# Feature blocks of the latents in another order, and queries and keys stored in DRAM by row tile

## The chip, the core and the metric

The kernel runs on one core of one Trainium2 chip. The metric is device time in microseconds (us); the figure for the kernel before is the median of three runs. Engines are named as in the profile: PE is TensorE's matmuls and PEld its weight loads, DVE is VectorE, ACT is ScalarE, POOL is GpSimd, SP is SyncE, which here only issues DMAs. PSUM banks hold 512 float32 columns on 128 partitions.

## The reference, cut to what matters

The model has two layers over 256 context tokens and 2048 latent tokens of width 1024, all in float32. The change touches the first (even) layer, up to its softmax attention:

```python
h  = rms_norm(x, norm_g[i]) * (1 + scale) + shift       # scale, shift from silu(c) @ ada_w + ada_b
hc = rms_norm(cx, norm_g[i]) * (1 + c_scale) + c_shift  # the context's own
lat = split_cols(jnp.dot(h, w_in), EVEN_SPLITS)         # 768 query latents, 256 key/value latents, 32 rotary key, ...
q = jnp.dot(rms_norm(q_lat, q_norm), w_uq)              # 8 heads of 64 plain and 32 rotary features
kv = jnp.dot(rms_norm(kv_lat, kv_norm), w_ukv)          # 8 heads of 64 key and 64 value features
k = concat(kv[..., :64], k_rope)                        # one rotary key for all heads
q, k = rms_norm(q, q_gain), rms_norm(k, k_gain)         # then axial rotation of the last 32
p = softmax(q @ k.T * scale)                            # 2048 queries on 2304 keys, 256 context queries on 256
```

Beside it the layer has a gated linear attention (GLA) on other columns of `w_in`, and a second (odd) layer with neighbourhood attention follows. The modulation of the second layer uses the same conditioning, so its rows (`ada_w[1]`) can be computed at any time.

## The kernel before, in words

Matmul operands are float32 values split into a high and a low part, and a full product is three matmuls: high by high, high by low, low by high. The 2304 tokens are 18 row tiles of 128 (`NT`; the first two are context). A list scheduler puts each engine's instructions in order from the order in which the program issues them, from dependences and from its own estimate of times; `issue_after` pins an instruction behind another one. Tiles come from pools by tag with a number of buffers (`bufs`), and a new tile waits until the old one with the same buffer is free. The profiled execution goes through these stages:

**Start** (0 to 37 us). The first modulation rows (`ada_first`), the first weights.

**The latents** (`even_latent`, lines 405 to 597; 37 to 347 us). The transposed input is worked in six feature blocks of tokens (`BLOCKS0`, line 403), 256, 256, 512, 512, 512 and 256 wide. For a block, `load` brings x; `stats` squares it on ACT (L108 is the helper of every ACT operation), POOL adds the squares, DVE adds the last one with the epsilon (line 435, tile acc), and one matmul with a matrix of ones (line 438, tile st) sums over partitions; ACT takes logarithm and exponential, DVE corrects the root (to line 446, tile R). `modulate` multiplies by R (line 458), applies scale and shift on ACT, splits into hhi and hlo (line 461). `block` multiplies two of the eight 128-column weights at a time (48 matmuls, line 487, tile gm, four banks). `evict` takes a result out: ACT copies the high part and squares, DVE forms the low part (line 502, tile lev, four buffers), and two DMAs write both to the DRAM array LT, the high part on ACT's queue and the low part on SP's. `rope_keys` makes the rotary key: eight products of 32 output columns (line 516, tile rp), which accumulate in pairs into four column groups of TensorE, over x, k and the weight Tr. `rows` turns the sums of squares and the rotary key into token rows (tile tp) with some DVE work. Block 0 goes one weight at a time. In the loop over blocks, `load(b + 2)`, `stats(b + 1)`, `modulate(b + 1)` and `rope_keys(b + 1)` are issued together after the first pair of weights of block b, and `rows(b)` at its end; the scheduler moves them from there.

In the same stage eight remaining modulation rows are made (`ada_steps`, line 276; eight jobs). A job streams 2 MB of `ada_w` through DVE in eight steps of two instructions (lines 286 and 288, tiles adac), then has two matmuls with a pick matrix (line 293, tile tp), and `ada_row` adds the bias row (tile adab) and turns or writes the result. From block 1 on, half a job is issued after each pair of weights, all behind the last load of x.

**The up-projection** (`even_up`, lines 599 to 736; 359 to 654 us). ACT and DVE first split the weights w_uq and w_ukv. Then for each row tile, `up(t)` multiplies the latents, read back from LT, normalises and rotates (tiles qn and kn), `fetch(t + 2)` loads ahead, and `fin(t - 2)` transposes queries and keys (line 701, four transposes per half tile of four heads), scales and splits them into the staging tile qkhl (ACT the high part through L108, DVE the low part, line 705), which has two buffers, and writes the halves to DRAM with three DMAs on SP's queue: high and low plain features (line 709) and both rotary parts. There are four half tiles per row tile (queries, keys; heads 0 to 3, 4 to 7). The arrays are QA and KA, (part, head, feature, token), and QC and KC, (head, part, feature, token), so a row of one feature is contiguous over tokens. At the end of the stage `fin` of the last two tiles runs beside products of the next stage (`first`).

**Maxima and the rest of w_in** (`even_rest` with `maxes`, lines 746 to 811; 654 to 1176 us). For each head, `mk` holds the high keys of all tokens and `mq` the queries of six tiles, each loaded by two DMAs; products (line 799, tile mx) and DVE maxima (line 800) run woven into big matmuls.

**Attention woven with GLA** (`even_attention`, lines 1108 to 1295; 1176 to 2000 us). SP loads keys (akh), low keys (akl), values and, per query block, queries (aq) through a helper `dma` (line 1120): five DMAs for a piece of keys, three for low keys, seven for a query block. GLA's loads (gu, line 889) stand in the same queue; POOL works on gu at line 851 and TensorE at 859.

**The odd layer** (2000 to 3663 us), which the change leaves alone.

These few lines carry the order and the writes (lines 583 to 592 and 707 to 711):

```python
                for n, ms in enumerate(groups):
                    block(b, sp, ms)
                    if b and n == 0:
...
                            r = stats(b + 1, sp)
                            modulate(b + 1, r)
                            rope_keys(b + 1, sp)
                    if b:
                        with self.tc.issue_after(self.xload.ins):
                            next(ada, None)
```

## Time and profile before

| | |
|---|---|
| median of 3 runs | 3670.68 us (3665.3 to 3672.92) |
| the profiled execution's own time | 3664.74 us |
| its span in the trace | 3662.9 us |
| mean granted clock of TensorE | 0.979 of full speed |
| DMA packets, bytes | 438411, 555.85 MB, mean 152 GB/s |
| HBM read, written | 354.09 MB, 198.17 MB |

The page first gives the busy time of each engine, then the span in 40 slices (here 91.6 us each), where a digit is the busy share in tenths; PEclk is the clock that the throttle granted to TensorE, also in tenths. A view by windows gives the busy time and the number of instructions of each engine in a stretch, then mean clock, DMA share and GB/s; it can be asked for one tile or line alone. In the view of waits a row "PE st L438 <- DVE acc L435: 8.1, 2, 4.9" reads: TensorE's instructions of line 438 stood 8.1 us in all for VectorE's line 435, two times, the longest 4.9 us. In a list of instructions the columns are start, duration, engine, line, operation, tiles and shapes, and with "x2" how many records there are in one row. An issue row of SPq gives how many DMAs, their time in the queue's engine (lowest, median and highest in ns), from when to when. A queue's row has packets, MB and the share of time of 16 DMA engines.

### The profile page before, as it was taken

What the parts mean: (1) busy time and instruction counts of PE and PEld (TensorE: products, weight loads), DVE (VectorE), ACT (ScalarE), POOL (GpSimd) and SP (SyncE); (2) the same over time, 40 slices, a digit from 0 to 9 for tenths busy, and PEclk for the clock granted to TensorE, in tenths of its full rate; (3) what the DMA queues carried; (4) which work ended last, traced back from release to release, by engine and by line L of the source; (5) the groups of instructions that cost most, each with busy time, mean ns of one, the idle gap of its engine ahead of it and who ended that gap; (6) DMA issues with size and microseconds to landing.
All of it is one profiled execution on the core that took longest, in us unless ns stands there. A gap on an engine that the chain in (4) does not pass through costs nothing. (4 is left out here: it accounts for less than half of the span.)

```text
span 3662.9 us, 53768 instructions
## 1 busy us (share of the span) xinstructions
PE 3514.9 (96%) x19388; PEld 2654.4 (72%) x19388; DVE 2374.6 (65%) x4649; ACT 1387.6 (38%) x2371; POOL 1305.7 (36%) x1382
## 2 busy tenths in 40 slices
PE   8898897999999999999999999999899999999899
PEld 5566776888888566666555887888788887655577
DVE  5774665688887577777885435444577784666732
ACT  5433444111111454455664214444432222555510
POOL 3223352010101133322220224333344442888863
PEclk9898998999999999999999999999999999999999
DMA  8565777322222434243533645455744446888672
GB/s 288 160 189 159 237 216 199 105 89 74 83 70 78 115 93 124 67 132 106 181 119 99 201 141 156 141 156 158 224 149 133 142 126 174 219 221 218 197 236 96
DMA packets 438411, 555.85 MB, mean 152 GB/s; under 512 B 36009, under 2 KB 313081, under 8 KB 431986
## 3 DMA queue, kind: packets, MB, share of 16 engines
q1 hardware_dynamic: 358130, 451.98, 42.1%
q0 software_dynamic: 22032, 63.00, 5.6%
q10 hardware_dynamic: 57984, 37.43, 3.3%
q8 instruction: 154, 2.52, 0.3%
q14 instruction: 111, 0.91, 0.1%
HBM read 354.09 MB, written 198.17 MB: 151 GB/s over the span
## 5 line engine op out<-in xcount | busy, mean ns | idle before, releaser
L800 DVE TENSOR_REDUCE mm<-mx 128x1 f32<-128x512 f32 (+1 forms) x656 | 389.5, 629 | 84.6 <-PE mx L799 76.7
L108 ACT ACTIVATE apt<-st 128x1024 f32<-128x1024 f32 (+1 forms) x296 | 300.0, 1014 | 315.1 <-PE st L1269 300.3
L1276 DVE TENSOR_TENSOR acc<-acc,apt 128x1024 f32<-128x1024 f32 x256 | 340.6, 1331 | 80.0 <-ACT apt L108 60.7
L1269 PE MATMUL st<-aq,akh 64*128 64x512 f32 x1728 | 313.6, 410 | 1.1 <-ACT apt L108 0.7
L1179 PE MATMUL av<-apt,av 128*64 128x512 f32 x1152 | 265.8, 598 | 0.0
L799 PE MATMUL mx<-mk,mq 96*128 96x512 f32 (+1 forms) x656 | 236.6, 374 | 3.2 <-DMA mq<-QC 3.2
L1766 POOL TENSOR_TENSOR oacc<-oacc,opt 128x576 f32<-128x576 f32 (+5 forms) x192 | 222.8, 1183 | 36.8 <-ACT rl L108 16.6
L1885 DVE TENSOR_TENSOR opt<-st,tab 128x64 f32<-128x64 f32 (+10 forms) x576 | 144.5, 317 | 140.1 <-PE st L1727 63.7
L1269 PE MATMUL st<-aq,akl 64*128 64x512 f32 (+1 forms) x1152 | 231.5, 392 | 0.0
L1269 PEld LDWEIGHTS st<-aq,akh 64*128 64x128 f32 x1728 | 153.7, 186 | 82.7 <-ACT apt L108 29.3
L1643 DVE CUSTOM_DVE_ANT_1 mx<-mx,mtab 128x217 f32<-128x217 f32 (+12 forms) x576 | 184.0, 338 | 39.7 <-PE mx L1637 30.5
L1179 PEld LDWEIGHTS av<-apt,av 128*64 128x64 f32 x1152 | 76.3, 136 | 135.3 <-issue 134.3
L108 ACT ACTIVATE u<-gm 128x352 f32<-128x352 f32 (+1 forms) x86 | 44.4, 517 | 334.2 <-PE gm L133 216.4
L108 ACT ACTIVATE opt<-opt 128x930 f32<-128x930 f32 (+8 forms) x130 | 104.3, 805 | 107.5 <-DVE opt L1885 102.8
L799 PEld LDWEIGHTS mx<-mk,mq 96*128 96x128 f32 x656 | 121.4, 188 | 15.0 <-issue 3.6
L1269 PEld LDWEIGHTS st<-aq,akl 64*128 64x128 f32 (+1 forms) x1152 | 112.8, 185 | 23.1
L131 PE MATMUL gm<-w1h,hhi 128*128 128x512 f32 x288 | 116.7, 405 | 7.4 <-ACT onat L108 7.4
L131 PE MATMUL gm<-w0h,hhi 128*128 128x512 f32 x288 | 116.2, 403 | 1.9 <-DVE hhi L353 1.9
L132 PE MATMUL gm<-w1l,hhi 128*128 128x512 f32 x288 | 115.3, 400 | 0.0
L133 PE MATMUL gm<-w1h,hlo 128*128 128x512 f32 x288 | 114.5, 398 | 0.0
L212 POOL TENSOR_TENSOR oss<-oss,mhalf 128x8 f32<-128x8 f32 x68 | 112.4, 1654 | 5.1
L133 PE MATMUL gm<-w0h,hlo 128*128 128x512 f32 x288 | 114.0, 396 | 0.0
(592 smaller groups left out, 9757.9 us busy)
## 6 DMA issues: line engine op xcount, KB each, us to landing
q<-Q SPq DMA_DIRECT2D x48, 512.0 KB
H<-x ACTq DMA_DIRECT2D x36, 512.0 KB
x<-H SPq DMA_DIRECT2D x34, 512.0 KB
wraw<-ada_w SPq DMA_DIRECT2D x64, 256.0 KB
wraw<-w_od SPq DMA_DIRECT2D x64, 256.0 KB
K1t<-okt POOLq DMA_DIRECT2D x32, 512.0 KB, 7.5
kt<-K1t SPq DMA_DIRECT2D x32, 512.0 KB
mtab<-rpb_q SPq DMA_DIRECT2D x16, 899.0 KB
```

The costliest lines, as they stand in the source:

```text
L108: return self.nc.scalar.activation(out, in_, func, **kw)
L131: self.nc.tensor.matmul(out, lh(k), rh(k), start=start and j == 0, stop=False)
L132: self.nc.tensor.matmul(out, lh(k), rl(k), start=False, stop=False)
L133: yield self.nc.tensor.matmul(out, ll(k), rh(k), start=False, stop=stop and j == n - 1)
L799: mm = nc.tensor.matmul(ps[:, :w], q[:A_QK, (t % 6) * P : (t % 6) * P + P], k[:A_QK, k0 : k0 + w], start=True, stop=True)
L800: nc.vector.tensor_reduce(out=m[:, t, n : n + 1], in_=ps[:, :w], axis=AX.X, op=ALU.max)
L1179: mm = nc.tensor.matmul(O[j, nb][i * 64 : i * 64 + 64, :w], V[j, kt // TT][:, kt % TT, i * 64 : i * 64 + 64], pts[:, i, :w], start=n == 0, ...
L1269: mm = nc.tensor.matmul(ps[:, o // 64, :w], k[o : o + r, kb, kq], Q[o : o + r, qb, :w], start=m == 0, stop=m == 4)
L1276: added = nc.vector.tensor_tensor(out=acc[:, :, :w], in0=a[:, :, :w], in1=pts[:, :, :w], op=ALU.add)
L1643: nc.vector.tensor_tensor_reduce(out=s, in0=s, in1=tb[:, ri : ri + rn, ci : ci + cn], scale=1.0, scalar=-3e38, op0=ALU.add, op1=ALU.max, a ...
L1766: self.psum = nc.gpsimd.tensor_tensor(out=a, in0=a, in1=pts[:, :, a0 - r0 : a1 - r0, :], op=ALU.add)
L1885: bias = nc.vector.tensor_tensor(out=pt[:, d[0], d[1]], in0=ps[:, d[0], d[1]], in1=tabs[j][i][:, ri : ri + rn, ci : ci + cn], op=ALU.add)
```

## The change

It has two parts.

**The latents.** The blocks are 256, 256, 256, 512, 512, 512 wide. `stats` becomes a generator with two stops: the squares and their sum for block b + 2 are issued after the second pair of weights of block b, and product, logarithm and correction after the third pair; R gets two buffers. `rows(b - 1)` and `modulate(b + 1)` are issued after the first pair, `rope_keys(b + 1)` after the third, `load(b + 2)` at the block's start; all of these are pinned behind the last matmul of the pair. The eight products of `rope_keys` are chained by `issue_after` in the order second half first, groups 3, 0, 1, 2. The modulation jobs are separate generators, and a list `turn` says after which pair of which block each starts (and the one before it ends); from block 0 to block 5 there are nine such places. The bias row of `ada_row` takes its tile from tag lev, which has four buffers, where it had its own.

**Queries and keys in DRAM.** QA, KA, QC and KC become one array QK with axes (queries or keys, row tile, half of the heads, feature, head, part, token in tile). A half tile's staging tile, 96 features by 4 KB, is written by one DMA. All reads go through a new helper `heads`, whose pieces are the 128 tokens of one tile, 512 bytes. `mk` and `mq` take one DMA where they took two, a piece of keys six where it took five, low keys four for three, a query block twelve for seven.

The diff, cut to its core:

```diff
-        br = self.tl(sp, [2, 512], "adab", bufs=1)
+        br = self.tl(sp, [2, 512], "lev", bufs=4)
...
-    BLOCKS0 = [(0, CTX), (CTX, 256), (512, 512), (1024, 512), (1536, 512), (2048, 256)]
+    BLOCKS0 = [(0, CTX), (CTX, 256), (512, 256), (768, 512), (1280, 512), (1792, 512)]
...
+                yield
...
-                r = self.tl(sp, [P, w], "R", bufs=1)
+                r = R[b] = self.tl(sp, [P, w], "R")
...
-                return r
+                yield
...
-            def modulate(b, r):
-                q0, w = self.BLOCKS0[b]
+            def modulate(b):
+                (q0, w), r = self.BLOCKS0[b], R.pop(b)
...
-                for h in range(2):
-                    for n in range(4):
-                        nc.tensor.matmul(ps[n * 32 : n * 32 + 32, :w], wr[:, h * 4 + n, :], xb[:, h * 4 + n, :w], start=h == 0, stop=h == 1)
+                mm = None
+                for h in (1, 0):
+                    for n in (3, 0, 1, 2):
+                        with self.tc.issue_after(mm.ins) if mm else ExitStack():
+                            mm = nc.tensor.matmul(ps[n * 32 : n * 32 + 32, :w], wr[:, h * 4 + n, :], xb[:, h * 4 + n, :w], start=h == 1, stop=h == 0)
...
-            ada = self.ada_steps([(0, 4), (0, 5)] + [(1, b) for b in range(6)], sp, pp, "tp")
+            jobs = [self.ada_steps([j], sp, pp, "tp") for j in [(0, 4), (0, 5)] + [(1, b) for b in range(6)]]
+            turn = [(0, 3), (1, 1), (2, 1), (3, 0), (3, 2), (4, 0), (4, 2), (5, 0), (5, 2)]
...
-            r = stats(1, sp)
-            modulate(1, r)
-            rope_keys(1, sp)
-            load(2)
+            for _ in stats(1, sp):
+                pass
+            modulate(1)
...
-                if b == 0:
-                    groups = [(m,) for m in range(M)]
-                else:
-                    groups = [(m, m + 1) for m in range(0, M, 2)]
+                groups = [(m, m + 1) for m in range(0, M, 2)]
+                if b + 2 < nb:
+                    load(b + 2)
...
-                    block(b, sp, ms)
-                    if b and n == 0:
-                        if b + 2 < nb:
-                            load(b + 2)
-                        if b + 1 < nb:
-                            r = stats(b + 1, sp)
-                            modulate(b + 1, r)
-                            rope_keys(b + 1, sp)
-                    if b:
-                        with self.tc.issue_after(self.xload.ins):
-                            next(ada, None)
-                rows(b, sp)
-            for _ in ada:
-                pass
+                    for g_ in ([(m,) for m in ms] if b == 0 else [ms]):
+                        mm = block(b, sp, g_)
+                    with self.tc.issue_after(mm.ins):
+                        if n == 0:
+                            if b:
+                                rows(b - 1, sp)
+                                if b + 1 < nb:
+                                    modulate(b + 1)
+                        elif n == 1 and b + 2 < nb:
+                            look[b] = stats(b + 2, sp)
+                            next(look[b])
+                        elif n == 2:
+                            if b + 2 < nb:
+                                next(look[b])
+                            if b + 1 < nb:
+                                rope_keys(b + 1, sp)
+                        if (b, n) in turn:
+                            i = turn.index((b, n))
+                            with self.tc.issue_after(self.xload.ins):
+                                if i:
+                                    next(jobs[i - 1])
+                                if i < len(jobs):
+                                    next(jobs[i])
+            rows(nb - 1, sp)
...
-        self.QA, self.KA = [self.scr(n, (2, A_HEADS, A_NOPE, T), F32) for n in ("QA", "KA")]
-        self.QC, self.KC = [self.scr(n, (A_HEADS, 2, A_ROPE, T), F32) for n in ("QC", "KC")]
+        self.QK = self.scr("QK", (2, NT, 2, A_QK, 4, 2, P), F32)
...
-                for z, (src, da, dc) in enumerate(((qn, self.QA, self.QC), (kn, self.KA, self.KC))):
+                for z, src in enumerate((qn, kn)):
...
-                        hs, ts = slice(h2 * 4, h2 * 4 + 4), slice(t * P, t * P + P)
-                        for part in range(2):
-                            nc.sync.dma_start(da[part, hs, :, ts].rearrange("h d t -> d h t"), hl[:A_NOPE, :, part, :].bitcast(F32))
-                        nc.sync.dma_start(dc[hs, :, :, ts].rearrange("h s d t -> d (h s) t"),
-                                          hl[A_NOPE:A_QK].rearrange("d h s t -> d (h s) t").bitcast(F32))
+                        nc.sync.dma_start(self.QK[z, t, h2].rearrange("d h s c -> d (h s c)"), hl[:A_QK].rearrange("d h s c -> d (h s c)").bitcast(F32))
...
-                    nc.sync.dma_start(k[:A_NOPE].bitcast(F32), self.KA[0, h])
-                    nc.sync.dma_start(k[A_NOPE:A_QK].bitcast(F32), self.KC[h, 0])
+                    self.heads(k[:A_QK], 1, h, 0, 0, NT)
...
-                            nc.sync.dma_start(q[:A_NOPE].bitcast(F32), self.QA[0, h, :, t * P : t * P + 768])
-                            nc.sync.dma_start(q[A_NOPE:A_QK].bitcast(F32), self.QC[h, 0, :, t * P : t * P + 768])
+                            self.heads(q[:A_QK], 0, h, 0, t, t + 6)
...
+    def heads(self, out, z, h, part, t0, t1, rows=slice(0, A_QK)):
+
+        src = self.QK[z, t0:t1, h // 4, rows, h % 4, part, :]
+        return self.nc.sync.dma_start(out.bitcast(F32).rearrange("d (t c) -> d t c", c=P), src.rearrange("t d c -> d t c"))
+
...
-                ts = slice(p * W + a, p * W + b)
-                dma(kh[:, 0, a:b], self.KA[0, 2 * j : 2 * j + 2, :, ts].rearrange("h d t -> (h d) t"))
+                ts = (p * W + a) // P, (p * W + b) // P
+                for i in range(2):
+                    self.heads(kh[i * 64 : i * 64 + 64, 0, a:b], 1, 2 * j + i, 0, *ts, nope)
...
-                        dma(kh[o : o + 32, 1, a:b], self.KC[2 * j + i, 0, :, ts])
+                        self.heads(kh[o : o + 32, 1, a:b], 1, 2 * j + i, 0, *ts, rope)
...
-                ts = slice(p * W + a, p * W + b)
-                dma(kl[:, 0, a:b], self.KA[1, 2 * j : 2 * j + 2, :, ts].rearrange("h d t -> (h d) t"))
+                ts = (p * W + a) // P, (p * W + b) // P
...
-                    dma(kl[i * 64 : i * 64 + 32, 1, a:b], self.KC[2 * j + i, 1, :, ts])
+                    self.heads(kl[i * 64 : i * 64 + 64, 0, a:b], 1, 2 * j + i, 1, *ts, nope)
+                    self.heads(kl[i * 64 : i * 64 + 32, 1, a:b], 1, 2 * j + i, 1, *ts, rope)
...
+            ts = q0 // P, (q0 + w) // P
...
-                dma(q[:, part, :w], self.QA[part, 2 * j : 2 * j + 2, :, qs].rearrange("h d t -> (h d) t"))
-            dma(q[:, 2, :w], self.QC[2 * j : 2 * j + 2, :, :, qs].rearrange("h s d t -> (h s d) t"))
+                for i in range(2):
+                    self.heads(q[i * 64 : i * 64 + 64, part, :w], 0, 2 * j + i, part, *ts, nope)
...
-                dma(q[i * 64 : i * 64 + 32, 3, :w], self.QC[2 * j + i, 0, :, qs])
+                for o, n, part in ((0, 2, 0), (32, 2, 1), (0, 3, 0)):
+                    self.heads(q[i * 64 + o : i * 64 + o + 32, n, :w], 0, 2 * j + i, part, *ts, rope)
```

More of the change, by code (lines that the diff above doesn't have):

```diff
@@ L410, in even_latent @@
         M = 8
-        kr, rs, x, hT, W, sums = {}, {}, {}, {}, {}, {}
+        kr, rs, x, hT, W, sums, R, look = {}, {}, {}, {}, {}, {}, {}, {}
         with ExitStack() as es:
@@ L486, in block @@
                             for i, (a, v) in enumerate(terms(*W[m], hT[b][h])):
-                                nc.tensor.matmul(p[:, :w], a[:, h * 4 + n, :], v[:, n, :w],
-                                                 start=(h, n, i) == (0, 0, 0), stop=(h, n, i) == (1, 3, 2))
+                                mm = nc.tensor.matmul(p[:, :w], a[:, h * 4 + n, :], v[:, n, :w],
+                                                      start=(h, n, i) == (0, 0, 0), stop=(h, n, i) == (1, 3, 2))
                 for p, m in zip(ps, ms):
                     evict(b, sp, m, p)
+                return mm
             def evict(b, sp, m, p):
@@ L556, in even_latent @@
                 load(0)
-                r = stats(0, st)
+                for _ in stats(0, st):
+                    pass
                 self.ada_first(st, pp, (("gm", 4), ("tp", 2)), stage)
@@ L566, in even_latent @@
                         nc.sync.dma_start(wr[:], self.i["w_rope"])
-                modulate(0, r)
+                modulate(0)
             sp = self.pool(es, "esT", bufs=2, side="left", reuse_waits="tile")
-            ada = self.ada_steps([(0, 4), (0, 5)] + [(1, b) for b in range(6)], sp, pp, "tp")
+            jobs = [self.ada_steps([j], sp, pp, "tp") for j in [(0, 4), (0, 5)] + [(1, b) for b in range(6)]]
+            turn = [(0, 3), (1, 1), (2, 1), (3, 0), (3, 2), (4, 0), (4, 2), (5, 0), (5, 2)]
             for m in range(4, M):
@@ L726, in even_up @@
                     fetch(s + 2)
-                if s >= NT:
+                else:
                     first(NT - 1, s - NT + 2)
                     first(NT - 2, s - NT + 2)
-                if 0 <= s - 2:
+                if s > 1:
                     fin(s - 2)
```

2 lines of the change are left out of this document (added).

## The prediction

> **What bounds the kernel now.** I read the page first, then the busy time by stage (the stages cut at the starts and ends of their matmuls), then the waits inside the stages that lose time.
>
> ```profile
> span 3662.9 us, 53768 instructions
> PE 3514.9 (96%) x19388; PEld 2654.4 (72%) x19388; DVE 2374.6 (65%) x4649; ACT 1387.6 (38%) x2371; POOL 1305.7 (36%) x1382
> PE   8898897999999999999999999999899999999899
> ```
>
> TensorE is busy 96% of the span, and the slices show that what is missing lies mostly in the first seven, about 640 us. By stage:
>
> ```profile
> core 0: us, PE busy (x) PEld busy (x) DVE busy (x) ACT busy (x) POOL busy (x), PEclk, DMA share, GB/s
> 36.97:347.18 310.21, 283.45 (x1398) 204.12 (x1398) 205.48 (x314) 129.63 (x247) 88.07 (x82) 0.93 0.59 173
> 347.18:359.17 11.99, 0.00 (x1) 0.00 (x1) 1.52 (x4) 1.94 (x3) 2.41 (x6) 0.50 0.91 345
> 387.88:597.41 209.53, 189.74 (x1037) 167.39 (x1037) 138.49 (x276) 97.68 (x164) 97.06 (x171) 0.98 0.78 223
> 597.41:653.98 56.57, 36.65 (x202) 32.34 (x201) 27.09 (x47) 20.48 (x31) 7.64 (x9) 0.82 0.77 199
> 653.98:1176.00 522.02, 521.47 (x2681) 460.12 (x2682) 427.90 (x717) 70.87 (x124) 51.75 (x89) 1.00 0.24 76
> 1176.00:1217.00 41.00, 32.10 (x201) 21.42 (x199) 14.51 (x20) 14.00 (x18) 7.80 (x15) 0.96 0.80 222
> 1217.00:2000.00 783.00, 778.74 (x5322) 476.04 (x5322) 589.57 (x647) 425.42 (x720) 215.39 (x196) 1.00 0.36 108
> ```
>
> The latents take the first row: 26.8 us without a matmul (310.21 - 283.45), and a granted clock of 0.93. Then TensorE stands still for 12.0 us. The up-projection takes the next two rows, its tiles 1 to 16 and its tail: idle 19.8 and 19.9 us, the tail at a clock of 0.82. The maxima (653.98 on) and the attention (1217 on) lose next to nothing; the attention's start loses 8.9 us. So everything that this change can win lies ahead of 654 us, and what it can lose lies behind. In the latents the waits are:
>
> ```profile
> PE gm L487 <- DVE lev L502: 8.4, 2, 5.7
> PE st L438 <- DVE acc L435: 8.1, 2, 4.9
> PE rp L516 <- ACT x L108: 5.1, 2, 4.7
> PE tp L293 <- DVE adac L288: 3.6, 2, 2.9
> ACT L108 <- PE st L438: 35.3, 4, 14.5
> ```
>
> TensorE arrives at the norm's product (st) before its sum is made, and at the rotary products (rp) before their input is modulated; ScalarE, in its turn, stands 35.3 us at the norm's logarithm, with evictions queued behind it. In the up-projection:
>
> ```profile
> PE tp L701 <- DVE qkhl L705: 27.8, 15, 7.0
> ACT qkhl L108 <- DMA QC<-qkhl: 54.2, 21, 6.0
> ACT qkhl L108 <- DMA KC<-qkhl: 26.2, 19, 5.9
> ```
>
> ScalarE waits 80.4 us for the writes of queries and keys to free one of two staging tiles; TensorE's transposes inherit 27.8 us of it.
>
> **The change, part by part.** The sum is made against the profiled execution, 3664.74 us (span 3662.9 and 1.84 around it). The median shown, 3670.68, is 5.94 higher; I carry the difference over unchanged.
>
> *A. Norms two blocks ahead.* Squares and sum are issued one group earlier than product, logarithm and correction, and both a block earlier than now. In the changed order the st product stands 12 or more gm matmuls behind where its sum can be ready, and rp after the third group. The two waits of 8.1 and 5.1 us go: **-13**. The bound is 0 if VectorE is late with the sum (rival 1).
>
> *B. Rotary products chained.* No operation is added. What one costs alone and side by side:
>
> ```profile
> 36.97:347.18 310.21, 29.94 (x80) 4.93 (x80) 2.93 (x6) 0.93 0.59 173
> 180.89 1.04 PE L516 MATMUL rp<-x,Tr 128*32 128x512 f32 x2
> 123.95 1.05 PE L516 MATMUL rp<-x,Tr 128*32 128x512 f32 x4
> ```
>
> The first row is the busy time of the rp tile alone. A product (two records) takes 1.04 us by itself, and two neighbours in different column groups take 1.05 together: they overlap. If all four groups do, eight 512-wide products take 2 x 1.05 = 2.1 us, and the 256-wide half; three wide and two narrow blocks make 3 x 2.1 + 2 x 1.05 = 8.4 instead of 29.9: 21.5 less. With only pairs overlapping it is about half, 13. I take **-17**; the lower bound is 0.
>
> *C. The clock.* The main products in this stage, and two clean stretches of them:
>
> ```profile
> 36.97:347.18 310.21, 225.62 (x1152) 182.23 (x1152) 26.36 (x48) 42.12 (x96) 0.93 0.59 173
> 128.00:150.00 22.00, 22.00 (x95) 17.67 (x95) 11.34 (x10) 6.86 (x12) 10.14 (x7) 1.00 0.67 213
> 328.00:344.00 16.00, 16.00 (x136) 16.00 (x135) 2.25 (x6) 3.29 (x10) 3.67 (x5) 1.00 0.29 83
> ```
>
> At full clock one is 22.00/95 = 0.232 us at 512 columns and 16.00/136 = 0.118 at 256. The stage has 576 of each, before and after the change (the blocks are only put in another order): 201.2 us. They took 225.6, so 24.4 us are the slow clock after stalls and the restarts between rp and gm. With two kinds of stall gone and the interleaving undone I take **-14** (0 to -24).
>
> *D. VectorE in the new order.* The ada sums (two instructions per 256 KB, line 288) start some 10 us earlier, ahead of the split of T7, and follow each other closely:
>
> ```profile
> L288 DVE SCALAR_TENSOR_TENSOR adac<-wraw,condT,adac 128x512 f32<-128x512 f32 x112 | 100.6, 936 | 16.2 <-DMA wraw<-ada_w 16.0
> L502 DVE TENSOR_TENSOR lev<-gm,lev 128x512 fp32r<-128x512 f32 x24 | 16.4, 682 | 9.8 <-ACT sq L108 6.8 <-ACT sumq L108 1.7 <-ACT sumkv L108 1.2
> L461 DVE TENSOR_TENSOR hlo<-x,hhi 128x512 fp32r<-128x512 f32 x24 | 15.2, 680 | 0.1
> L458 DVE TENSOR_TENSOR x<-x,R 128x512 f32<-128x512 f32 x24 | 14.7, 678 | 0.0
> L286 DVE TENSOR_SCALAR adac<-wraw,condT 128x512 f32<-128x512 f32 x16 | 10.7, 676 | 38.0 <-DMA wraw<-ada_w 19.4 <-PE tp L293 18.6
> ```
>
> A job is 14 x 0.936 + 2 x 0.676 = 14.5 us. Block 3 holds two: 29, with 8 evictions (5.5), 16 instructions that modulate block 4 (10.9) and some 4 for block 5's norm: 49 us. TensorE's share is 192 x 0.232 = 44.5 and about 5 of small products. Blocks 1 and 2 have about 29 and 32 against some 26 each. So VectorE has no slack from block 1 to block 3, and catches up in 4 and 5. A job also holds one of the four eviction tiles (its bias row has moved there), so ScalarE's evictions can queue behind it, and TensorE behind its banks. The waits of 8.4 and 3.6 us stay, and I add **+5** (0 to +20).
>
> *E. Queries and keys, writing.* Three DMAs become one per half tile, twelve become four per row tile.
>
> ```profile
> L709 SPq DMA_DIRECT2D QA<-qkhl x72: 574/581/1905, 395.8 to 639.4; - x72
> L620 SPq DMA_DIRECT2D lth<-LT x18: 327/424/1320, 346.3 to 582.1; - x18
> L1120 SPq DMA_DIRECT2D akh<-KC x52: 302/412/1447, 1176.6 to 1797.1; - x52
> q1 hardware_dynamic: 54254, 46.55, 77.5%
> ```
>
> An issue of 256 pieces holds SP for 0.58 us, one of 128 for 0.42. Twelve make 7.0 us, with the three other DMAs of a tile 8.4, against a pace of 209.53/16 = 13.1 us a tile; after the change four of 96 pieces, 1.7 with the same three 3.1. The bytes stay the same, 46.55 MB in 77.5% of 16 x 209.53 us, or 17.9 bytes per ns and engine; I count nothing for larger pieces. The single write waits for VectorE's half (0.75 us later than the first write now); the shorter issue covers that. What is late next is TensorE itself. Of 19.8 us idle I take **-15** (0 to -24, with the clock).
>
> *F. The tail.* The last eight half tiles follow the same ring with little else to do, so each wait shows. 56.57 - 36.65 = 19.9 us idle and some 10 lost to the clock; about half goes: **-14** (-4 to -25). The 12.0 us ahead of the stage depend on the loads of w_uq, which stand where they stood: 0.
>
> *G. Reading.* Rows of 1.5 to 9 KB become 512-byte pieces, and a query block takes 12 DMAs instead of 7.
>
> ```profile
> q10 hardware_dynamic: 37648, 18.75, 21.3%
> 1176.22 0.34 SPq L1120 DMA_DIRECT2D akh<-KA  x1
> 1208.19 1.24 SPq L889 DMA_DIRECT2D gu<-Un  x2
> PE gl L859 <- POOL gu L851: 7.3, 1, 7.3
> ```
>
> ScalarE's queue in the latents writes almost only 512-byte pieces: 18.75 MB in 21.3% of 16 x 310.21 us, 17.7 bytes per ns, as good as 17.9 above. So bytes cost the same. Issues don't: by 0.42 us for 128 pieces and 0.58 for 256 (0.75 for 384, extended), the train from 1176.2 until the gate's loads rises from about 17 to 28 us of issue. It took 32 us, so part of the extra is hidden by the DMA engines; TensorE's wait of 7.3 us at its end grows: **+8** (0 to +13). Later trains stand behind attention that runs 778.74 of 783.00 us: 0, and +10 if that cover fails.
>
> The Trainium skill, DMA: Bandwidth & Descriptors, section Bandwidth, advises batches of 1 MiB and calls transfers under 64 KB dominated by descriptors; by it the finer reads would be dear. The rates above, 17.7 against 17.9, don't show it.
>
> Sum: -13 - 17 - 14 + 5 - 15 - 14 + 8 = **-60**: 3664.74 - 60 = 3604.7 profiled, and 3670.68 - 60 = **3610.7**, rounded 3610.
>
> **The rivals.**
>
> *1. VectorE sets the pace of the latents.* For it: D's 49, 32 and 29 us against 50, 26 and 26, in-order. Against it: over the stage it is busy 205.5 of 310 us. Then A and C go and D costs 12: -17 + 12 - 15 - 14 + 8 = -26, 3645.
>
> *2. Landing, not issue, holds the staging tiles.* Waits of up to 6.0 us on a write that is issued in 0.58 speak for it; against it, that SP is busy issuing for 8.4 of 13.1 us. Then E and F give nothing: -31, 3640. The Trainium skill, same page, section on the anatomy of one DMA, has about 2 us per DMA, mostly for the receipt of the write; by that rule fewer issues would help little. The rows can't part the two yet.
>
> *3. SP in the attention (slower).* The same lists as in G give about 12 us more issue for each of four head pairs. If the gate's loads, behind them in the one queue, come late by all of it at TensorE, and each stop costs some 4 us of clock more, 4 x 16 = 64 us. Against A to F, -68, that is still no loss; with SP's wait on full rings, which stretched 17 us of issue to 32 above, doubling it (4 x 32 = 128) the time is 3730. It decides from 17 us a pair. Against it: that stage now has 4.3 us idle in 783.
>
> **How the numbers follow.** Forecast 0.58; rival 1 0.12; rival 2 0.11; everything at its better bound (near 3570) 0.05; rival 3 0.09; gains and losses cancel 0.05. A difference of 0.2% (7.3 us) is about what a measurement of this kernel can tell from no change. Faster is the sum of the first four, 0.86; same 0.05; slower 0.09. The bounds summed run from 3564 to 3698; the range leaves out the far ends: **3570 to 3655**.
>
> **What would show it.** Right: the first matmul of the up-projection some 40 us earlier, rp in runs of eight, no ScalarE wait on st; qkhl's waits on DMA less than half of 80; the maxima start near 585 instead of 654. Wrong: PE waits on adac or lev of over 20 us (1), a pace still near 13 us a tile (2), idle TensorE with late gu or aq behind 1217 us (3).

## The result, and the profile after

The changed kernel takes 3644.48 us (median of four runs, 3642.0 to 3651.78) against 3671.38 of before (four runs; the 3670.68 above is the median of three of them): ratio 0.9933, 95% interval 0.9914 to 0.9952, or 24.6 us less (18 to 32). The direction was as forecast and the range of 3570 to 3655 holds the time, near its upper end; the size was not: 60 us were forecast, and less than half of them came. Below, a kernel's gain in us is (1 - ratio) x 3671; the interval of most kernels is 6 to 8 us to each side.

The page of the changed kernel:

```profile
span 3640.2 us, 53542 instructions
PE 3492.4 (96%) x19388; PEld 2653.6 (73%) x19388; DVE 2378.7 (65%) x4649; ACT 1386.5 (38%) x2371; POOL 1315.5 (36%) x1382
PE   7998997999998999999999999999899999999999
```

TensorE is as busy in share as before, and most of the weak slices are still among the first seven. By stage, before from the up-projection on (the first two rows stand in the prediction), then after. The columns are the stretch and its length, then busy time by engine:

```profile
359.17:653.98 294.81, 248.70 (x1312) 217.56 (x1312) 180.52 (x340) 130.59 (x211) 114.63 (x202) 0.92 0.76 216
653.98:1177.90 523.92, 523.37 (x2689) 461.64 (x2690) 429.55 (x720) 71.47 (x125) 51.75 (x89) 1.00 0.25 76
1177.90:1987.70 809.80, 796.65 (x5459) 488.09 (x5459) 595.90 (x657) 434.55 (x732) 221.90 (x210) 1.00 0.38 114
1987.70:3662.90 1675.20, 1637.93 (x8420) 1273.18 (x8420) 952.72 (x2587) 599.90 (x1016) 818.20 (x771) 0.99 0.59 172
```

```profile
36.90:321.97 285.07, 260.92 (x1402) 204.69 (x1398) 206.40 (x314) 127.77 (x247) 94.48 (x82) 0.95 0.66 195
321.97:329.80 7.83, 0.00 (x1) 0.00 (x1) 1.73 (x4) 1.94 (x3) 3.10 (x6) 0.50 0.89 330
329.80:610.80 281.00, 242.32 (x1312) 213.89 (x1312) 180.03 (x340) 130.40 (x212) 118.38 (x203) 0.94 0.71 226
610.80:1135.70 524.90, 523.00 (x2690) 461.59 (x2691) 429.23 (x720) 71.02 (x124) 51.20 (x88) 1.00 0.26 76
1135.70:1958.60 822.90, 800.70 (x5459) 488.37 (x5459) 596.06 (x657) 434.69 (x733) 219.85 (x210) 0.99 0.42 113
1958.60:3640.20 1681.60, 1642.68 (x8420) 1275.81 (x8420) 956.05 (x2587) 600.84 (x1016) 819.72 (x771) 0.99 0.59 171
```

| stage | forecast | measured |
|---|---|---|
| latents | -39 | 310.2 to 285.1: -25.1 |
| gap before the up-projection | 0 | 12.0 to 7.8: -4.2 |
| up-projection with its tail | -29 | 294.8 to 281.0: -13.8 |
| maxima | 0 | +1.0 |
| attention | +8 | 809.8 to 822.9: +13.1 |
| the rest, untouched | 0 | 1675.2 to 1681.6: +6.4 |

The last row is a warning. Over the fourteen profiles of this study, all with the same code there, that stretch takes 1675.2 to 1692.9 us: 1675 to 1683 in the four with the old DRAM layout and 1676 to 1693 (mean 1685) in the ten with the new one. Whether the layout has a part in this is not settled here. The latents repeat better: where their code is the same, their last product starts at 321.2 to 325.1 us in six kernels. The up-projection does not. From its first product to the first maximum, the seven kernels that have the changed kernel's code there take 274.4 to 288.2 us, and the three with the code of before take 291.9 to 298.4. A difference of a few us in that stage, read from one profile each, cannot be told from scatter.

Where TensorE waits in the latents now, and what ScalarE waits for in the up-projection:

```profile
PE gm L488 <- DVE lev L504: 9.3, 3, 4.8
PE st L439 <- DVE acc L435: 5.0, 3, 2.4
PE rp L520 <- ACT x L108: 3.7, 1, 3.7
PE tp L293 <- DVE adac L288: 3.4, 2, 2.7
PE tp L533 <- POOL sumkv L507: 2.2, 1, 2.2
```

```profile
ACT qkhl L108 <- DMA QK<-qkhl: 76.5, 39, 4.8
```

The names are those of before, and so nearly are the sums: TensorE stands 285.07 - 260.92 = 24.2 us in the stage where it stood 26.8. ScalarE's wait for the writes, 80.4 before, is 76.5. What TensorE inherits of it at the transposes fell by more, from 27.8 to 17.6:

```profile
PE tp L714 <- DVE qkhl L718: 17.6, 10, 5.5
```

In the latents, what did shrink is the rotary tile (first row; 29.94 before) and a little of the main products (second row; 225.62 before):

```profile
36.90:321.97 285.07, 10.48 (x84) 2.62 (x80) 2.90 (x6) 0.95 0.66 195
36.90:321.97 285.07, 220.40 (x1152) 183.44 (x1152) 26.38 (x48) 42.04 (x96) 0.95 0.66 195
```

So the latents' 25.1 are 19.5 from rp, 5.2 from gm, 2.6 from waits, and +2 or so in the small rest.

### The profile page after: what moved, and what is told of

It reads as the page before. It is cut to its first block, busy times and chain, and to the rows that moved or that the text cites. A ratio compares the mean times of both kernels' runs of the same rounds, so it can differ in the third digit from the quotient of the medians.

```text
span 3640.2 us, 53542 instructions
## 1 busy us (share of the span) xinstructions
PE 3492.4 (96%) x19388; PEld 2653.6 (73%) x19388; DVE 2378.7 (65%) x4649; ACT 1386.5 (38%) x2371; POOL 1315.5 (36%) x1382
```

## The experiments

**The two parts by themselves.** One kernel takes the functions of the latents from before and all from `even_up` on from the changed kernel; the other the reverse.

```diff
 (from the change's diff: every hunk from even_up on)
-        self.QA, self.KA = [self.scr(n, (2, A_HEADS, A_NOPE, T), F32) for n in ("QA", "KA")]
-        self.QC, self.KC = [self.scr(n, (A_HEADS, 2, A_ROPE, T), F32) for n in ("QC", "KC")]
+        self.QK = self.scr("QK", (2, NT, 2, A_QK, 4, 2, P), F32)
...
```

> The kernel before with the new DRAM layout alone (one write per half tile, reads by 512-byte pieces); the latents are those of before. Theory from the trace of the changed kernel: the up-projection gains 9.8 us and its tail 4.3, the start of the attention gives 12.4 back, so 2 us less than before, about 3669, with ScalarE still waiting about 75 us for the writes. Rival (the sizes of the forecast, issue on SP holds the staging tiles): -15 - 14 + 8 = -21, about 3650, and the wait falls under 40 us.

Measured: ratio 0.9985 (0.9974 to 0.9996), 5.5 us less. The stage from first product to first maximum takes 643.4 - 362.0 = 281.4 us as in the changed kernel, and ScalarE's wait is what it was:

```profile
ACT qkhl L108 <- DMA QK<-qkhl: 80.2, 42, 4.8
```

Twelve issues became four, and ScalarE's wait stayed. TensorE's share of it fell from 27.8 to 20.8 us, and the stage is 13.4 us shorter than before, where E and F had 29. The forecast's sizes for E and F fall.

```diff
 (from the change's diff: ada_row, BLOCKS0 and even_latent)
-    BLOCKS0 = [(0, CTX), (CTX, 256), (512, 512), (1024, 512), (1536, 512), (2048, 256)]
+    BLOCKS0 = [(0, CTX), (CTX, 256), (512, 256), (768, 512), (1280, 512), (1792, 512)]
...
```

> The kernel before with the new order of the latents alone; QA, KA, QC, KC as before. Theory: the two parts do not touch each other, the latents end 25 us earlier and the gap for w_uq is 4 us shorter, so 29 us less, about 3642. Rival: part of the gain of the up-projection in the changed kernel came from the latents, and then this kernel gains 35 or more, about 3636.

Measured: 0.9931 (0.9914 to 0.9947), 25.3 us less, near the theory's 29; the latents' last product starts at 321.8, the stage behind it takes 628.4 - 330.0 = 298.4 us as in the old kernel (294.8). The two gains sum to 30.8 us where both together gave 24.6, within the intervals; no more than that can be said of the parts touching each other.

**Staging tiles.** The wait goes with the number of tiles or with the bytes, and a third tile tells which.

```diff
-                        hl = self.tl(sp, [P, 4, 2, P], "qkhl", F32R, bufs=2)
+                        hl = self.tl(sp, [P, 4, 2, P], "qkhl", F32R, bufs=3)
...
-                sq = self.tl(sp, [P, Q_LORA], "sql", bufs=1)
+                sq = self.tl(pp, [P, 2, 512], "sql", bufs=1)
...
```

> The changed kernel with three staging tiles qkhl instead of two; for the room, the squares of queries and keys (sql) are written to two free PSUM banks, and two small constants lie in another pool. Theory (a write's landing of about 4 us holds the two tiles, the issue on SP never did): ScalarE's wait for the writes falls from 76 to under 35 us, and the up-projection with its tail becomes 8 to 15 us shorter, about 3633. Rival (the writes are limited by the bytes that the 16 DMA engines move in this stage): the wait stays above 60 us and the time within 4 us of 3644.

Measured: 0.9824 (0.9803 to 0.9846), 64.6 us less than before, 40 less than the changed kernel. The wait and the stage:

```profile
ACT qkhl L108 <- DMA QK<-qkhl: 31.1, 12, 4.4
PE tp L714 <- DVE qkhl L718: 8.2, 6, 3.0
```

```profile
334.30:594.30 260.00, 237.98 (x1311) 216.79 (x1312) 176.96 (x340) 128.69 (x212) 117.78 (x203) 0.95 0.76 247
```

281.0 became 260.0, more than the 8 to 15 expected and clear of the 274 to 288 of the same stage with two tiles. It moved 247 GB/s where two tiles moved 226, so the bytes of the stage as a whole were not the limit. The two profiled executions differ by 20.4 us, the size of this stage; the medians by more, since the profiled execution was the slowest of its four here and the fastest there.

The control keeps `bufs=2` and takes the second edit alone:

> The changed kernel with the squares in PSUM and the two constants in the other pool, as in the kernel with three staging tiles, but with two staging tiles. Theory: the third tile did all of that gain, so this one takes the changed kernel's time, 3640 to 3650, with a wait of about 75 us on the writes. Rival: the squares in PSUM take work off the path of ScalarE and VectorE, and this kernel has a third or more of the gain, 3632 or less.

Measured: 0.9913 (0.9894 to 0.9932), 3642.96 us; the stage takes 614.5 - 331.9 = 282.6 us and the wait is 78.2. The squares' place does nothing in this stage; the third tile did it.

Both edits put into the kernel with the new latents and the old arrays:

> The new latents with the old DRAM layout (twelve writes per row tile, the old reads), and three staging tiles. Theory (landing holds the tiles, not issue, and the old layout's 8.4 us of issue fit into a pace of 12 us a tile): from the first matmul of the up-projection to the first of the maxima 260 to 268 us, as in the changed kernel with three tiles, and with the cheaper start of the attention the time is about 10 us less than that kernel's. Rival (with landing out of the way the twelve issues set the pace): 275 us or more, and the time is equal or above that kernel's.

Measured: 0.9843 (0.9827 to 0.9858), 57.6 us less; the stage:

```profile
331.50:602.40 270.90, 241.76 (x1312) 217.49 (x1313) 176.90 (x340) 128.16 (x212) 116.01 (x203) 0.94 0.85 237
```

270.9 lies between the theory's 268 and the rival's 275. Most of the gain comes without the new layout (298.4 to 270.9). With three tiles too, the stage is 11 us shorter with the single write (260.0 against 270.9), about as much as with two (13.4). These are single profiles of a stage that scatters by 14 us, so the 11 is rough. In the whole the two layouts with three tiles are equal within the intervals (57.6 and 64.6 us less): what the new one wins in writing, its attention gives back (823.2 us against 811.6).

**The rotary products.** Chaining alone, put into the kernel before:

```diff
-                for h in range(2):
-                    for n in range(4):
...
+                for h in (1, 0):
+                    for n in (3, 0, 1, 2):
+                        with self.tc.issue_after(mm.ins) if mm else ExitStack():
...
```

> The kernel before with nothing but the eight rotary products chained in their new order. Theory: the busy time of the rp tile falls from 29.9 to about 10.5 us and the time by nearly as much, -17 to -20, about 3653, since TensorE is the engine that is late in the blocks after the first. Rival: VectorE sets the pace of the blocks, the time that TensorE saves turns into waits on lev, acc and adac, and the kernel gains under 8 us, 3663 or more.

Measured: 0.9962 (0.995 to 0.9974), 14.0 us less (10 to 18): between the two, nearer the theory. The busy time of rp falls from 29.9 to 9.3. TensorE's waits on lev rise from 8.4 to 13.1, those on adac from 3.6 to 7.6, and one of 6.1 on ScalarE's hhi is new, while those on acc and x fall from 13.2 to 5.8: the other engines take back a part. And the reverse, the same lines undone in the changed kernel:

> The changed kernel with the eight rotary products in their old order and not chained. Theory (the products overlap only when they stand side by side, and the time on TensorE counts): rp takes 25 us or more again and the latents are 12 to 18 us longer, 3656 to 3662. Rival (VectorE's pace hides what TensorE saves): the latents are under 5 us longer.

Measured: 0.9938 (0.9916 to 0.9959), which is the changed kernel's ratio; the latents' last product starts at 323.6 instead of 321.6. The theory falls here, by its premise. The row of the rp tile:

```profile
36.90:322.00 285.10, 15.93 (x80) 3.29 (x80) 2.90 (x6) 0.95 0.65 192
```

So rp takes 15.9 us and not 25. In the new order of issue the products are pinned behind a pair of weights, and the scheduler puts many of them side by side without a chain. So what bought the time was that they stand together; the chain is one way to it, the place of issue another.

**VectorE's load and queue.** Six lines of VectorE's time in the changed kernel show the wait of 4.8 us on lev (start, length, line):

```profile
62.54 0.95 DVE L462 TENSOR_TENSOR hlo<-x,hhi 128x256 fp32r<-128x256 f32 x1
63.41 4.60 DVE L288 SCALAR_TENSOR_TENSOR adac<-wraw,condT,adac 128x512 f32<-128x512 f32 x4
67.93 0.41 DVE L504 TENSOR_TENSOR lev<-gm,lev 128x256 fp32r<-128x256 f32 x1
68.27 0.41 DVE L435 SCALAR_TENSOR_TENSOR acc<-sq,acc 128x256 f32<-128x256 f32 x1
68.60 0.41 DVE L504 TENSOR_TENSOR lev<-gm,lev 128x256 fp32r<-128x256 f32 x1
77.09 0.43 DVE L445 TENSOR_TENSOR sq<-st,R 128x256 f32<-128x256 f32 x1 [8.07 <-ACT R L108]
```

Block 0's products end at 63.65, and block 1's wait until 68.40 for a bank: the eviction stands behind 4.6 us of a modulation job that has been put ahead of it. At 69 the next stall of the same kind begins: VectorE stands 8.07 us at the norm's correction, in its fixed order, with evictions behind it. Until 72.39 the norm's product waits its turn in TensorE's order, behind the products that had stood for the bank. The next 4 us are ScalarE's, and 2.6 of them are two instructions ACT_TABLE_LOAD of 1.28 us each, one ahead of the logarithm and one ahead of the exponential.

A stop also costs clock. The two rows are TensorE right after the stop that ends at 68.40:

```profile
68.40:71.30 2.90, 2.90 (x13) 2.90 (x14) 0.61 (x2) 0.66 (x2) 0.00 (x0) 0.50 1.06 397
71.50:75.90 4.40, 4.40 (x37) 4.35 (x36) 0.00 (x0) 2.81 (x4) 0.00 (x0) 1.00 0.54 171
```

The granted clock is 0.50 for 2.9 us and 1.00 from 71.5 on, so this stop of 4.8 us costs about 1.5 us more (an estimate, half of 2.9). After the next one, of 3.9 us, the clock is 0.50 for 4.5 us. By blocks (1, 3 and 5):

```profile
63.65:104.70 41.05, 31.74 (x227) 29.33 (x227) 27.75 (x51) 20.29 (x48) 17.90 (x18) 0.88 0.68 209
133.45:202.30 68.85, 60.45 (x254) 40.23 (x253) 58.31 (x82) 39.76 (x68) 27.84 (x21) 0.95 0.74 217
262.00:315.00 53.00, 53.00 (x227) 39.66 (x226) 27.75 (x38) 8.69 (x16) 10.73 (x10) 0.97 0.48 138
```

VectorE is busy 58.3 of 68.9 us in block 3 and half of block 5. Two kernels test this. In one, the sums after the first eighth are made for one column:

```diff
-                        nc.vector.scalar_tensor_tensor(out=a[:], in0=w[:], scalar=self.condT[:, k, c : c + 1], in1=a[:],
+                        nc.vector.scalar_tensor_tensor(out=a[:, :1], in0=w[:, :1], scalar=self.condT[:, k, c : c + 1], in1=a[:, :1],
```

> The changed kernel, in which the sums of the eight modulation rows after the first eighth of the input are made for one column out of 512 (so the later rows are not those of the reference); loads, matmuls and order of issue are kept, and VectorE has about 90 us less to do in the latents. Theory (VectorE has no slack in blocks 0 to 3, and its queue makes TensorE wait): the 21 us of TensorE waits on lev, acc, x and adac go, with some of the slow clock after them, and the latents take 255 to 265 us instead of 285, about 3618. Rival (the waits come from the order in which st and its successors stand, not from VectorE's load): the latents take 278 or more, about 3638.

Measured: 0.988 (0.9864 to 0.9897), 44 us less than before, 19 less than the changed kernel. VectorE's load falls to 138 us and the latents to 272:

```profile
37.10:309.00 271.90, 256.34 (x1402) 205.40 (x1398) 138.01 (x314) 128.80 (x247) 80.95 (x82) 0.96 0.67 203
```

```profile
PE gm L488 <- DVE lev L504: 11.3, 5, 3.9
```

That is half of the theory. The waits on acc, x and adac are gone, 12 us in sum; those on lev are not: with only 138 of 272 us busy, VectorE still makes TensorE wait, because an instruction that waits holds up the evictions behind it. The longest of these waits, 3.9 us to 77.29, ends with an eviction that stood behind the norm's correction, which itself had waited 4.9 us for ScalarE, and behind eight instructions that modulate. Load and order share the blame. In the other kernel the jobs start later and more evenly:

```diff
-            turn = [(0, 3), (1, 1), (2, 1), (3, 0), (3, 2), (4, 0), (4, 2), (5, 0), (5, 2)]
+            turn = [(1, 2), (2, 2), (3, 1), (3, 3), (4, 1), (4, 3), (5, 0), (5, 2), (5, 3)]
```

> The changed kernel with the eight modulation jobs starting later and spread evenly, the first after the third pair of weights of block 1 instead of the fourth of block 0, one and a half jobs in block 3 instead of two, more in blocks 4 and 5. Theory (VectorE's load and the jobs' place in its queue in blocks 0 to 3 make TensorE wait): the waits of 4.8 and 3.9 us on lev in block 1 go, and the latents end 8 to 14 us earlier, about 3633. Rival: the sums meet the same evictions later, the latents end within 4 us of 322, and the time stays near 3644.

Measured: 0.9894 (0.9863 to 0.9924), 3632.2 us, 14 us below the changed kernel by the ratios, though the intervals overlap. In the profile the latents' last product starts 2.6 us earlier and the first of the up-projection 6.2 us earlier (323.6); the waits on lev come to 11.3 us, the longest 5.8 in block 3; those on acc and x fall from 8.7 to 0.8, and those on adac and sumkv rise from 5.6 to 9.7. So the rival's reading of the latents is the better one: the sums meet evictions elsewhere. The rest of the gain lies in the stage behind (598.0 - 323.6 = 274.4 us), and it cannot be told from scatter.

**The norm's place.** The changed kernel with the norm issued for block b + 1 just before its modulation, as before:

```diff
+                                    for _ in stats(b + 1, sp):
+                                        pass
                                     modulate(b + 1)
-                        elif n == 1 and b + 2 < nb:
-                            look[b] = stats(b + 2, sp)
-                            next(look[b])
...
```

> The changed kernel with the norm issued one block ahead again (squares, product and correction for block b + 1 just before its modulation), all else as changed. Theory (VectorE's queue, not the place of the norm, sets the waits, so A of the forecast bought little): the latents end within 5 us of 322, and the time is 3644 to 3650. Rival (A holds as forecast): the waits on acc and x come back, the latents take 10 to 15 us more, and the time is 3655 or more.

Measured: 0.9935 (0.9913 to 0.9957), the changed kernel's ratio. In the profile, which caught the slowest of its five executions, the latents' last product starts at 329.1, 7.5 us later: between the two bounds. The waits on acc are 6.9 us instead of 5.0, those on x 1.0 instead of 3.7, and waits of 7.0 us on hhi are new. The look-ahead is worth some 7 us there, half of A, and it does not show in the time above the scatter.

**The attention's start.** SP begins this stage with a train, an unbroken run of loads of keys, values and queries, and the loads for GLA's gate (the last is gu) stand behind it. With these it takes 33 us before and 43 after. TensorE's wait at the gate for gu was 7.3 us before; after the change the waits there are:

```profile
PE gl L866 <- POOL gu L858: 13.5, 1, 13.5
PE gl L876 <- DVE gw L1044: 3.0, 1, 3.0
```

SP's DMA queue in 34 us of the train before, and then in 36 us of it after:

```profile
q1 hardware_dynamic: 5949, 6.69, 75.2%
```

```profile
q1 hardware_dynamic: 11752, 5.61, 70.0%
```

By the first, 6.69 MB in 75.2% of 16 x 34 us are 16.4 bytes per ns and engine, in packets of 1.1 KB on the mean; by the second, 5.61 MB in 70.0% of 16 x 36 us are 13.9, in packets of 0.5 KB. So here the finer reads also move at 15% less. Issuing the gate's loads from GpSimd's queue takes them past the train:

```diff
-        nc.sync.dma_start(raw[:97], self.i["gate_w"])
+        nc.gpsimd.dma_start(raw[:97], self.i["gate_w"])
...
```

> The changed kernel with the gate's first loads (gate_w, tri, halves, gla_norm and the first two rows of glr) issued by GpSimd's queue instead of standing behind the train of key and query loads on SP's. Theory (the extra issues of the train delay these loads): TensorE's wait of 13.5 us for gu at the start of the attention falls below 3, and the kernel gains 9 to 14 us, about 3633. Rival (the DMA engines are full in this stretch and land them no earlier): the wait stays above 9 us, 3641 or more.

Measured: 0.9925 (0.9906 to 0.9944), 3647.29 us, no gain that shows. The wait on gu is gone, so the loads do land early, and another has taken its place:

```profile
PE gl L876 <- DVE gw L1044: 8.4, 1, 8.4
```

gw needs a small copy that was still issued on SP behind the train. The stage falls from 822.9 to 817.9 us only. Half right: the cause was the queue, but there were two waits in it.

**All together,** three staging tiles, the even jobs, the gate's loads, and the copy of gw on GpSimd's queue as well:

```diff
...
-        nc.sync.dma_start(gw[97:98].bitcast(F32), gw[96:97].bitcast(F32))
+        nc.gpsimd.dma_start(gw[97:98].bitcast(F32), gw[96:97].bitcast(F32))
```

> The changed kernel with three staging tiles, the evenly spread modulation jobs, and the gate's first loads and its small copy gw on GpSimd's queue. Theory (three separate stages, so the gains add): 32 to 40 us from the staging tile, 12 from the jobs and 8 to 14 from the start of the attention, below the changed kernel, so 82 to 92 us below before. Rival (they meet the same DMA engines): 70 us or less below before.

Measured: 3596.34 us, 0.9783 (0.9764 to 0.9802), 79.7 us less than before (73 to 87). Latents, up-projection and attention:

```profile
36.90:318.20 281.30, 261.38 (x1402) 206.85 (x1398) 204.02 (x313) 128.70 (x247) 91.47 (x82) 0.94 0.68 202
322.80:578.90 256.10, 235.92 (x1312) 216.22 (x1312) 176.41 (x340) 129.05 (x212) 115.21 (x204) 0.95 0.77 250
1101.50:1908.70 807.20, 798.58 (x5459) 488.12 (x5459) 596.11 (x657) 434.82 (x732) 224.64 (x217) 1.00 0.42 115
```

As far as the intervals tell, the gains add: the up-projection is 24.9 us shorter than in the changed kernel, and the attention, at 807.2, below before's 809.8. The sum is just short of the 82 expected, and the interval holds it.

## Why the prediction was wrong in size

**E and F, the writing: wrong in mechanism.** The step that failed is "the shorter issue" as what holds the staging tiles: -15 and -14 were taken, and -13.8 in all came (9.7 ahead of the tail's first product, at 606.2 before and 567.1 after, and 4.1 behind it). SP's issue did fall, to

```profile
L720 SPq DMA_DIRECT2D QK<-qkhl x72: 303/320/1078, 368.9 to 600.6; - x72
```

four times 0.32 us, or 1.3 a row tile where 1.7 was worked out, instead of 7.0. ScalarE's wait went from 80.4 to 76.5 only. In the tail the turns of the two tiles can be read off ScalarE and VectorE:

```profile
586.91 0.68 ACT L108 ACTIVATE qkhl<-tp,qkg 96x512 fp32r<-96x512 f32 x1 [0.26 <-DMA QK<-qkhl]
592.35 0.68 ACT L108 ACTIVATE qkhl<-tp,qkg 96x512 fp32r<-96x512 f32 x1 [4.75 <-DMA QK<-qkhl]
593.28 0.68 ACT L108 ACTIVATE qkhl<-tp,qkg 96x512 fp32r<-96x512 f32 x1 [0.25 <-DMA QK<-qkhl]
598.15 0.68 ACT L108 ACTIVATE qkhl<-tp,qkg 96x512 fp32r<-96x512 f32 x1 [4.18 <-DMA QK<-qkhl]
```

```profile
587.16 1.40 DVE L718 SCALAR_TENSOR_TENSOR qkhl<-tp,qkg,qkhl 96x512 fp32r<-96x512 f32 x2
593.07 0.75 DVE L718 SCALAR_TENSOR_TENSOR qkhl<-tp,qkg,qkhl 96x512 fp32r<-96x512 f32 x1 [4.51 <-ACT qkhl L108]
```

VectorE ends the first tile of a pair at about 587.9, and the tile comes back at 592.35, 4.4 us later. In the next turn it ends at 593.82 and the tile is back at 598.15: 4.3 us, of which 0.3 are issue, and here no load stands ahead of the writes. The DMA engines' busy share from 593.5 to 598.5, in slices of 0.125 us, splits these 4.3 us:

```profile
DMA  0000000009899787799669996976973200000000
```

They stand still for 0.8 us, move the 786 KB of the pair's two writes for 2.9 us, and the tile is free 0.65 us after that. So two tiles turn in some 5.8 us (592.35 to 598.15), and for half of it the DMA engines stand idle, waiting for the next pair. A third tile lets a write start in that time (21 us of the stage).

This is rival 2, named with a chance of 0.11 and 3640. Its argument, waits of 6.0 us on a write issued in 0.58, was the stronger row, and it was there to be read. The Trainium skill's rule that was put beside it (DMA: Bandwidth & Descriptors, anatomy of one DMA: about 2 us fixed, mostly the write's receipt, there for DMAs issued by GpSimd) points the same way; here, on SP's queue, some 1.5 of the 4.3 us lie outside the moving. The chance was set by the sum of SP's issue (8.4 of 13.1 us busy), which is a share, not a wait. The price was set on TensorE's whole idle time, 19.8 and 19.9 us, while the shown row gave it 27.8 us in both for these tiles, of which 10.2 went. That E and F would give nothing, as rival 2 has it, was too low: layout_only ties 13.4 us to the layout. Whether they come from the shorter issue, from the larger pieces or from one DMA for three, no run parts.

**B, the rotary products: right in the overlap.** -17 forecast, -19.5 in rp's busy time. Eight 512-wide products overlap in all four groups:

```profile
183.34 1.92 PE L520 MATMUL rp<-x,Tr 128*32 128x512 f32 x16
```

1.92 us against 2 x 1.05 worked out. By itself in the old kernel it was worth 14 us of time. That the chain brings it holds only there: in the changed kernel rp falls to 15.9 us without a chain, which adds 5.5 of the 19.5.

**A, C and D, waits and clock of the latents: mis-sized, and half by the mechanism of rival 1.** "The two waits of 8.1 and 5.1 us go: -13": they became 5.0 and 3.7, with 1.0 more on sumkv; the idle time fell by 2.6 where A and D together gave 8. C was to follow them: gm fell by 5.2, not 14, since stops remained, and after one the granted clock is 0.50 for some us (2.9 and 4.5 in the two cases above). ScalarE's wait on st, which was to vanish, is 13.3 us where it was 35.3. The bound named for A, 0 "if VectorE is late with the sum", is nearer to what came than -13. D's estimate that VectorE has no slack from block 1 to 3 fits block 3 (58.3 of 68.9 us busy). What the forecast did not see is VectorE's order: ada_light takes 68 us of its load away, and the waits on lev stay.

That rival 1's number, 3645, is the time that came is luck. It has -5 for the latents, where -25.1 came, and leaves E and F at -29, where -13.8 came; the errors cancel.

**The gap of 12.0 us: 4.2 were won** where 0 was forecast. The gap is about 8 us in the kernel with the new latents alone and 12 in that with the chain alone, so it goes with the new order of the latents. What in that order shortens it was not tested.

**G, the reading: right in kind, too small.** +8 forecast, +13.1 came, at the upper end of 0 to +13: 9.0 of it is idle TensorE and 4.1 busy time. The train is 10 us longer as worked out (11), TensorE's wait on gu 6.2 longer, and a wait just behind it (1.6 us before, on rT) is 3.0 on gw. "So bytes cost the same" rested on a rate of 512-byte writes; the reads of the train came 15% slower. Rival 3 did not happen: TensorE's waits on key and query loads come to 1.1 us in the whole stage, all within the train. Two of its terms have no row. What it calls SP's wait on full rings is named in none: of the 33 us before, 5.8 are waits of SP for buffers, and why the issues took longer is open. And its 4 us of clock for each stop is more than the stop at 68.40 cost (1.5).

Summed, in the profiled executions: of 37 us too much, 14 are A, C and D, 15 E and F, 5 G, 7 the maxima and the untouched rest, which the scatter of that rest covers, less 4 for the gap. The stated bounds add up to 3700 at the upper end (3710 if the cover of the later trains fails), not 3698; nothing hangs on it.

## What to carry to other kernels

Where an engine waits on a DMA to free a buffer, compare each wait with the issue time of one DMA and with its time to land. If each wait is several times an issue, add a buffer before you save issues, and price the change by what the bottleneck engine inherits of the wait. Time that is saved on one engine is worth less while another engine, working in a fixed order, holds the evictions: the chain took 20.6 us off the rotary products and 14.0 off the kernel. Read that engine's queue around each wait, and look at what stands ahead of the instruction waited for. And a load queue that is made longer delays everything behind it, each of the small loads of the next stage included.

## What the runs showed of the hardware

Matmuls of 32 output columns in four column groups overlap when they stand side by side: eight of 512 columns take 1.92 us, and one alone 1.04. An SP issue of 96 pieces of 4 KB costs 0.32 us, one of 256 pieces of 512 bytes 0.58. A write of 384 KB from a staging tile, with a second one right behind it, gave its buffer back 4.3 us after its data were ready; the DMA engines moved the two for 2.9 us of that. After TensorE had stood for 4.8 and 3.9 us, its granted clock was 0.50 for 2.9 and 4.5 us. SP's queue, reading in packets of 0.5 KB on the mean, moved 13.9 bytes per ns and engine in the attention's start, against 16.4 in packets of 1.1 KB there, though writes of 512-byte pieces in the latents had run at 17.7.
